# A 3x3 convolution by Winograd rows: four products in five lower halves, and the differences on VectorE

## The chip, the core and the metric

The kernel runs on one core of a Trainium2 chip. Its time is the device time of one execution in microseconds (us). Of the engines, TensorE (PE) multiplies matrices from SBUF into PSUM; VectorE (DVE), ScalarE (ACT) and GpSimd (POOL) work elementwise; SyncE (SP) issues all transfers between HBM and SBUF, which 16 DMA engines carry. A "half" below is 32 of the 64 output rows of a pair of images.

## The reference

The output is the 3x3 convolution of 16 images of 64 channels and 64x64 pixels with 128 filters, padded with one row and column of zeros, all in float32:

```python
x_pad = np.pad(x, ((0, 0), (0, 0), (1, 1), (1, 1)), mode='constant')
...
output[b, co] += weight[co, ci, kh, kw] * x_pad[b, ci, kh:kh+h, kw:kw+w]
```

## The kernel before

Two images make a pair: their 2 x 64 channels fill the 128 partitions, so eight pairs (`p` = 0 to 7) are worked on, each in two halves (`h` = 0 the upper, 1 the lower), sixteen halves in a row (the loop at the end of the function). Each half gives two blocks of 8 row pairs: the block F (rows 16 to 31 in the upper half, 32 to 47 in the lower) and the block G (rows 0 to 15, or 48 to 63).

Rows are combined as in Winograd's scheme for two output rows of a three-tap filter. With two neighbouring input rows b (even) and c (odd), the kernel makes in float16 the sums b+c ("ss", `sums`, L108), the differences c-b ("dd", `diffs`, L115) and the differences of the rows on both sides ("ee", `outers`, L125). The weights are combined once, at the start, into seven sets (`Wt`, L88 on): G0, G1, G2 are the three filter rows, HP and HM half of (G0 + G2) plus and minus half of G1, G01 is G0-G1, G21 is G2-G1. A product is six matrix multiplications: three column taps for each of the two images (`mms`, L162); each is of 64 input channels, and the two images' run side by side.

Block F of each half takes four products (HP on ss, HM on dd, G0 on ee, G2 on ee). Block G takes five: G1 on ss, and four on "xh", a plain float16 copy of 17 rows that ScalarE makes (`cast`, L138): G01 and G2 into one PSUM tile, G21 and G0 into another. So a half has nine products, 54 multiplications.

The four PSUM tiles of a half are pf1, pg1, pf2 and pg2, and these are all there are: the next half uses the same four again in the same order. ScalarE copies the first products out to the output rows (L247, L249, L251); when the later products have been added in PSUM, VectorE adds or subtracts the tile to those rows (L258 frees pg2, L259 frees pf1, L260 frees pf2), and ScalarE copies pg1 (L261).

The order on each engine is that of the program's text (`keep` holds every instruction in its place). GpSimd makes sums, differences and outers of the half after next (`transforms`, called with n + 2); only the very first half's are VectorE's. ScalarE makes the cast of the next half after its three copies. The buffers of "ss" and "dd" are four, those of "xh" three, and those of "ee" two, one for each pair.

SBUF holds eleven "homes" of one 64x64 row image a partition (L51 on). All inputs are loaded at the start, by SyncE, in the order of the pairs. The outputs of a pair take two homes, some of them the pair's own input home, some that of an earlier output, which must have been stored (`O_HOME`). Home 6, the second of pair 2 and of pair 3, is such a one.

`stores` (L213) issues the stores, all on SyncE's queue. Nothing is stored before half (2, 0) is done; then four parts and pairs 0, 1 and 2 follow, and from pair 3 on each pair after its lower half, both images in one transfer (`store_both`). Pair 5 is an exception: its first image goes in one transfer, rows 0 to 56 of the second in another, and its last seven rows in two, of 124 channels and of 4.

Of the kernel before, what the change touches and what calls it, by code (L numbers as in the profile page):

```python
# [9 lines left out]
F16 = mybir.dt.float16  # L10
# [5 lines left out]
def kernel(  # L16
# [12 lines left out]
    nc = tc.nc  # L29
    B, CI, H, W = x.shape  # L30
    CO = weight.shape[0]
    assert H == 64 and W == 64 and CI == 64 and CO == 128 and B == 16
    NP = B // 2
    RB = 8

    keep = tc.keep_in_program_order
# [8 lines left out]
    cpool = ctx.enter_context(tc.tile_pool(name="cpool", bufs=3))  # L45
# [7 lines left out]
    xs = [homes[:, k, :, :] for k in X_HOME]  # L53

    def out_homes(p):
        lo, hi = O_HOME[p]
        return homes[:, lo : hi + 1 : hi - lo, :, :]
# [29 lines left out]
    G0, G1, G2, G21, G01, HP, HM = range(7)  # L87
# [4 lines left out]
    def wrow(i):  # L92
        return Wt[:, i, :, :].rearrange("p t c -> p (t c)")
# [8 lines left out]


    F_BLK, G_BLK = (1, 2), (0, 3)
    C_ROW = (0, 47)
    tr = {}

    def sums(eng, p, h):  # L108
        v = xs[p].rearrange("p (j i) c -> p j i c", i=2)
        t = tpool.tile([128, 16, W], F16, tag="ss", name="ss")  # L110
        j = 16 * h
        keep(eng.tensor_add(t, v[:, j : j + 16, 0, :], v[:, j : j + 16, 1, :]))  # L112
        return t

    def diffs(eng, p, h):  # L115
        v = xs[p].rearrange("p (j i) c -> p j i c", i=2)
        t = tpool.tile([128, RB, W], F16, tag="dd", name="dd")
        j = RB * F_BLK[h]
        keep(eng.tensor_sub(t, v[:, j : j + RB, 1, :], v[:, j : j + RB, 0, :]))  # L119
        return t  # L120

# [3 lines left out]
    def outers(eng, p, h):  # L125
        if h == 0:
            ees[p] = epool.tile([128, 32, W], F16, tag="ee", name="ee")
        lo, hi = (16, 33) if h == 0 else (33, 48)
        keep(
            eng.tensor_sub(  # L130
                ees[p][:, lo - 16 : hi - 16, :],
                xs[p][:, lo - 1 : hi - 1, :],
                xs[p][:, lo + 1 : hi + 1, :],
            )
        )
        return ees[p]

    def cast(p, h):  # L138
        t = cpool.tile([128, 17, W], F16, tag="xh", name="xh")
        keep(nc.scalar.copy(t, xs[p][:, C_ROW[h] : C_ROW[h] + 17, :]))  # L140
        return t

    def transforms(eng, p, h):
        return sums(eng, p, h), diffs(eng, p, h), outers(eng, p, h)

    xh = {}
    keep(nc.scalar.mul(g0h, wps[0], 0.5))  # L147
    keep(nc.scalar.copy(wrow(G0), wps[0]))
# [2 lines left out]
    keep(nc.scalar.copy(wrow(G1), wps[1]))  # L151
    s0 = sums(nc.vector, 0, 0)
    keep(nc.vector.scalar_tensor_tensor(wrow(HM), wps[1], -0.5, th, MULT, ADD))
    d0 = diffs(nc.vector, 0, 0)
    xh[0, 0] = cast(0, 0)
    keep(nc.vector.tensor_sub(wrow(G01), wps[0], wrow(G1)))
    keep(nc.scalar.copy(wrow(G2), wps[2]))
    keep(nc.vector.tensor_sub(wrow(G21), wps[2], wrow(G1)))
    tr[0, 0] = s0, d0, outers(nc.vector, 0, 0)
    tr[0, 1] = transforms(nc.gpsimd, 0, 1)  # L160

    def mms(tiles, terms, start, stop):  # L162
        n = 3 * len(terms)
        i = 0
        for wi, src, row in terms:
            for kw in (1, 0, 2):
                c_lo, c_hi = max(0, 1 - kw), min(W, W + 1 - kw)
                lo, hi = 0, RB
                at, step, rows = row
                while at + step * lo < 0:  # L170
                    lo += 1
                while at + step * (hi - 1) > rows - 1:
                    hi -= 1
                first, last = at + step * lo, at + step * (hi - 1)
                for b2 in range(2):
                    p0 = 64 * b2
                    keep(
                        nc.tensor.matmul(  # L178
                            tiles[:, b2, lo:hi, c_lo:c_hi],
                            Wt[p0 : p0 + 64, wi, kw, :],  # L180
                            src[
                                p0 : p0 + 64,
                                first : last + 1 : step,
                                c_lo + kw - 1 : c_hi + kw - 1,
                            ],
                            start=start and i == 0,
                            stop=stop and i == n - 1,
                            skip_group_check=not start,
                        )
                    )  # L190
                i += 1

    def acc():
        return psum.tile([128, 2, RB, W], F32, tag="acc", name="acc")

    halves = [(p, h) for p in range(NP) for h in range(2)]

    def store(p, b2, lo=0, hi=H, c=0, n=CO):
        keep(
            nc.sync.dma_start(  # L200
                out[2 * p + b2, c : c + n, lo:hi, :], out_homes(p)[c : c + n, b2, lo:hi, :]
            )
        )

    def store_both(p):
        pair = out[2 * p : 2 * p + 2, :, :, :].rearrange("b c h w -> c b h w")
        keep(nc.sync.dma_start(pair, out_homes(p)))

    FEW = 57

    def stores(p, h):  # L213
        if (p, h) == (2, 0):
            store(2, 1, 0, 32)
            store(0, 0)
        elif (p, h) == (2, 1):
            store(2, 1, 32, H)
            store(0, 1)
            store_both(1)  # L220
            store(2, 0)
        elif (p, h) == (5, 1):
            store(5, 0)
            store(5, 1, 0, FEW)
            store(5, 1, FEW, H, 0, 124)
            store(5, 1, FEW, H, 124, 4)
        elif p > 2 and h == 1:
            store_both(p)

    for n, (p, h) in enumerate(halves):  # L230
        if n + 2 < len(halves):
            tr[halves[n + 2]] = transforms(nc.gpsimd, *halves[n + 2])
        if h == 0:
            both = out_homes(p)
            ov = both.rearrange("p b (j i) c -> p b j i c", i=2)
        ss, dd, ee = tr.pop((p, h))
        xc = xh.pop((p, h))
        jf, jg = RB * F_BLK[h], RB * G_BLK[h]
        sf, sg = jf - 16 * h, jg - 16 * h
        g_at = 2 * jg - C_ROW[h]  # L240


        f0, f1 = (ov[:, :, jf : jf + RB, i, :] for i in range(2))
        g0, g1 = (ov[:, :, jg : jg + RB, i, :] for i in range(2))
        pf1, pg1, pf2, pg2 = acc(), acc(), acc(), acc()
        mms(pf1, [(HP, ss, (sf, 1, 16))], True, True)
        keep(nc.scalar.copy(f1, pf1))  # L247
        mms(pg1, [(G1, ss, (sg, 1, 16))], True, True)
        keep(nc.scalar.copy(g1, pg1))  # L249
        mms(pf2, [(HM, dd, (0, 1, RB))], True, True)  # L250
        keep(nc.scalar.copy(f0, pf2))  # L251
        if n + 1 < len(halves):
            xh[halves[n + 1]] = cast(*halves[n + 1])
        mms(pg2, [(G01, xc, (g_at, 2, 17)), (G2, xc, (g_at + 2, 2, 17))], True, True)
        mms(pf1, [(G0, ee, (16 * h, 2, 32))], False, True)
        mms(pg1, [(G21, xc, (g_at + 1, 2, 17)), (G0, xc, (g_at - 1, 2, 17))], False, True)
        mms(pf2, [(G2, ee, (16 * h + 1, 2, 32))], False, True)
        keep(nc.vector.tensor_add(g1, pg2, g1))  # L258
        keep(nc.vector.tensor_add(f0, pf1, f0))  # L259
        keep(nc.vector.tensor_sub(f1, f1, pf2))  # L260
        keep(nc.scalar.copy(g0, pg1))  # L261
        stores(p, h)


# [28 lines left out]
```

## Time and profile before

| what | value |
|---|---|
| median of 3 runs | 126.45 us (126.12 to 126.69) |
| the profiled execution | 126.43 us |
| its span, first to last instruction | 124.56 us |
| PE busy | 96.4 us, 77% of the span |
| DVE busy | 64.0 us, 51% |
| ACT busy | 81.3 us, 65% |
| POOL busy | 90.4 us, 73% |
| queue of SyncE's transfers | 50.63 MB, 96.6% of 16 engines' span |
| HBM | 17.07 MB read, 33.55 MB written |

The span is what the profile shows of the execution; the time around it belongs to the execution, not to an instruction. "Busy" is the time in which an engine had an instruction at work. In the profile's lines "out<-in" names the program's tiles, L178 is line 178 of the kernel, and a line like "9.44 2.34 POOL L112" in a timeline gives start, duration, engine and line. Instructions of VectorE, ScalarE and GpSimd overlap a little with the next one of their engine, so the spacing of their starts is somewhat below the duration shown. Where the prediction speaks of the packet list, it means the single DMA packets in the trace, with start, duration and size; packets of 4 bytes signal the end of a transfer's share on one DMA engine.

### The profile page before, as it was taken

To read this page: it belongs to the slowest core of one execution; us is meant where nothing else is said; L and a number is where in the kernel's file an instruction comes from. 1 tells how busy PE (TensorE), PEld (TensorE's weight loads), DVE (VectorE), ACT (ScalarE), POOL (GpSimd) and SP (SyncE) were. 2 spreads that over 40 slices of the span, in tenths; PEclk is the share of its full clock that TensorE was granted. 3 is DMA by queue.
4 is the path that set the end of the run, shared out by engine and by line. 5 is a ranking of instruction groups with operands and counts; after the bars stand their busy time and mean duration, and the time that the engine had idled before them with its cause. 6 is when DMAs were issued, how large, how long until landed. Compare 5 with 4: busy or idle time off the path is not lost.

```text
span 124.6 us, 2115 instructions
## 1 busy us (share of the span) xinstructions
PE 96.4 (77%) x873; PEld 50.0 (40%) x873; DVE 64.0 (51%) x56; ACT 81.3 (65%) x86; POOL 90.4 (73%) x52
## 2 busy tenths in 40 slices
PE   0339999999999999969999999999999996000000
PEld 0213555555545544534555555555555552000000
DVE  0199666473939381907384938566573939000000
ACT  4456688888797947749979796988888793000000
POOL 2209999999999999999999999999999600000000
PEclk9999999999999999999999999999999999855555
DMA  4999999999999999999999999999999999999981
GB/s 123 359 455 426 426 447 421 416 442 426 426 431 421 408 445 424 431 429 426 431 434 413 437 421 434 416 431 426 437 421 427 419 390 422 421 421 442 437 374 68
DMA packets 3954, 50.77 MB, mean 408 GB/s; under 512 B 360, under 2 KB 488, under 8 KB 744
## 3 DMA queue, kind: packets, MB, share of 16 engines
q1 hardware_dynamic: 3944, 50.63, 96.6%
q8 instruction: 7, 0.11, 0.3%
q14 instruction: 3, 0.02, 0.0%
HBM read 17.07 MB, written 33.55 MB: 406 GB/s over the span
## 4 chain that ended last, share of the span: by engine, by line
PE 68%; DMA 11%; DVE 3%; ACT 2%; SPq 0%; issue 0%; ACTq 0%
PE acc L178 68%; DMA out_dram<-homes 6%; DMA homes<-in_x_dram 5%; DVE homes L260 2%; DVE ss L112 1%; ACT homes L247 1%; ACT homes L249 1%; SPq L66 0%; ACTq L247 0%; SPq L200 0%
## 5 line engine op out<-in xcount | busy, mean ns | idle before, releaser
L178 PEld LDWEIGHTS <-Wt 64*128 64x128 f16 x864 | 49.0, 96 | 49.9 <-issue 6.8
L178 PE MATMUL acc<-xh,Wt 64*128 64x504 f16 (+3 forms) x384 | 46.3, 372 | 0.2
L112 POOL TENSOR_TENSOR ss<-homes 128x1024 f16<-128x1024 f32 x15 | 35.4, 2360 | 5.1 <-DMA homes<-in_x_dram 5.1
L258 DVE TENSOR_TENSOR homes<-acc,homes 128x1024 f32<-128x1024 f32 x16 | 19.6, 1224 | 35.3 <-PE acc L178 23.9
L130 POOL TENSOR_TENSOR ee<-homes 128x960 f16<-128x960 f32 (+1 forms) x15 | 35.2, 2349 | 0.0
L178 PE MATMUL acc<-ee,Wt 64*128 64x504 f16 (+1 forms) x192 | 26.5, 377 | 1.2 <-ACT homes L247 1.1
L178 PE MATMUL acc<-ss,Wt 64*128 64x504 f16 (+1 forms) x192 | 24.9, 392 | 2.6 <-DVE ss L112 2.6
L261 ACT COPY homes<-acc 128x1024 f32<-128x1024 f32 x16 | 16.3, 1016 | 9.7 <-PE acc L178 9.7
L247 ACT COPY homes<-acc 128x1024 f32<-128x1024 f32 x16 | 16.2, 1012 | 9.7 <-PE acc L178 5.2
L119 POOL TENSOR_TENSOR dd<-homes 128x512 f16<-128x512 f32 x15 | 20.0, 1337 | 0.0
L260 DVE TENSOR_TENSOR homes<-homes,acc 128x1024 f32<-128x1024 f32 x16 | 19.5, 1219 | 1.0 <-PE acc L178 0.2
L259 DVE TENSOR_TENSOR homes<-acc,homes 128x1024 f32<-128x1024 f32 x16 | 19.4, 1214 | 0.0
L140 ACT CAST xh<-homes 128x1088 f16<-128x1088 f32 x16 | 17.9, 1119 | 0.0
L251 ACT COPY homes<-acc 128x1024 f32<-128x1024 f32 x16 | 16.5, 1030 | 0.3 <-PE acc L178 0.3
L249 ACT COPY homes<-acc 128x1024 f32<-128x1024 f32 x16 | 16.3, 1017 | 0.3 <-PE acc L178 0.3
L178 PE MATMUL acc<-dd,Wt 64*128 64x504 f16 (+1 forms) x96 | 13.9, 392 | 0.0
L101 PE MATMUL wp<-homes 128*128 128x128 f16 x9 | 1.2, 310 | 4.5 <-POOL homes L84 4.5
L149 DVE SCALAR_TENSOR_TENSOR homes<-wp,homes 128x384 f32<-128x384 f32 x1 | 0.6, 557 | 5.6 <-ACT homes L147 5.6
L130 DVE TENSOR_TENSOR ee<-homes 128x1088 f16<-128x1088 f32 x1 | 2.8, 2812 | 0.0
L101 PEld LDWEIGHTS <-homes 128*128 128x128 f16 x9 | 0.9, 159 | 4.5 <-POOL homes L84 4.5
L84 POOL CAST homes<-homes 128x576 f16<-128x576 f32 x1 | 0.7, 662 | 2.4 <-DMA homes<-in_weight_dram 2.4
L85 ACT CAST homes<-homes 128x576 f16<-128x576 f32 x1 | 0.7, 671 | 1.7 <-DMA homes<-in_weight_dram 1.7
(17 smaller groups left out, 8.2 us busy)
## 6 DMA issues: line engine op xcount, KB each, us to landing
out_dram<-homes SPq DMA_DIRECT2D x5, 4096.0 KB, 20.9
homes<-in_x_dram SPq DMA_DIRECT2D x7, 2048.0 KB, 30.3
out_dram<-homes SPq DMA_DIRECT2D x4, 2048.0 KB, 16.4
out_dram<-homes SPq DMA_DIRECT2D x2, 1024.0 KB, 6.5
out_dram<-homes SPq DMA_DIRECT2D x1, 1824.0 KB, 20.5
homes<-in_x_dram SPq DMA_DIRECT2D x1, 1088.0 KB, 5.8
homes<-in_x_dram SPq DMA_DIRECT2D x1, 960.0 KB, 7.6
homes<-in_weight_dram SPq DMA_DIRECT2D x1, 288.0 KB, 2.9
```

The costliest lines, as they stand in the source:

```text
L112: keep(eng.tensor_add(t, v[:, j : j + 16, 0, :], v[:, j : j + 16, 1, :]))
L119: keep(eng.tensor_sub(t, v[:, j : j + RB, 1, :], v[:, j : j + RB, 0, :]))
L130: eng.tensor_sub(ees[p][:, lo - 16 : hi - 16, :], xs[p][:, lo - 1 : hi - 1, :], xs[p][:, lo + 1 : hi + 1, :],)
L140: keep(nc.scalar.copy(t, xs[p][:, C_ROW[h] : C_ROW[h] + 17, :]))
L178: nc.tensor.matmul(tiles[:, b2, lo:hi, c_lo:c_hi], Wt[p0 : p0 + 64, wi, kw, :], src[p0 : p0 + 64, first : last + 1 : step, c_lo + kw - 1 : ...
L247: keep(nc.scalar.copy(f1, pf1))
L249: keep(nc.scalar.copy(g1, pg1))
L251: keep(nc.scalar.copy(f0, pf2))
L258: keep(nc.vector.tensor_add(g1, pg2, g1))
L259: keep(nc.vector.tensor_add(f0, pf1, f0))
L260: keep(nc.vector.tensor_sub(f1, f1, pf2))
L261: keep(nc.scalar.copy(g0, pg1))
```

## The change

In the lower halves of pairs 2 to 6 (`FOUR`) block G takes four products as block F does: HP on ss, HM on its own differences, and G0 and G2 on outer differences of rows 47 to 64. These outer differences lie in the "xh" tile, and VectorE makes them (`last_outers`), with the last row as a plain copy. ScalarE makes no cast for such a half, copies all four first products out, and VectorE adds or subtracts all four tiles.

The differences c-b of all halves are VectorE's now, and no longer GpSimd's. They are queued for the next half (`others`) ahead of the work of the present one, so ahead of its additions and subtractions.

The stores of pair 5 are two, one an image, and so are those of pairs 6 and 7; pairs 3 and 4 keep one transfer for both images.

```diff
+    FOUR = ((2, 1), (3, 1), (4, 1), (5, 1), (6, 1))
...
+    def last_outers(eng, p):
+
+        t = cpool.tile([128, 17, W], F16, tag="xh", name="xh")
+        keep(eng.tensor_sub(t[:, 0:15, :], xs[p][:, 47:62, :], xs[p][:, 49:64, :]))
+        keep(eng.tensor_copy(t[:, 15, :], xs[p][:, 62, :]))
+        return t
+
     def transforms(eng, p, h):
-        return sums(eng, p, h), diffs(eng, p, h), outers(eng, p, h)
-
+        return sums(eng, p, h), outers(eng, p, h)
+
+    def others(p, h):
+
+        dd[p, h] = [diffs(nc.vector, p, F_BLK[h])]
+        if (p, h) in FOUR:
+            dd[p, h].append(diffs(nc.vector, p, G_BLK[h]))
+            xh[p, h] = last_outers(nc.vector, p)
...
-        elif (p, h) == (5, 1):
-            store(5, 0)
-            store(5, 1, 0, FEW)
-            store(5, 1, FEW, H, 0, 124)
-            store(5, 1, FEW, H, 124, 4)
+        elif p in (5, 6, 7) and h == 1:
+            store(p, 0)
+            store(p, 1)
         elif p > 2 and h == 1:
             store_both(p)
...
+        four = (p, h) in FOUR
+        if n + 1 < len(halves):
+            others(*halves[n + 1])
...
-        mms(pg1, [(G1, ss, (sg, 1, 16))], True, True)
+        mms(pg1, [(HP if four else G1, ss, (sg, 1, 16))], True, True)
...
-        if n + 1 < len(halves):
+        if four:
+            mms(pg2, [(HM, ds[1], (0, 1, RB))], True, True)
+            keep(nc.scalar.copy(g0, pg2))
+        if n + 1 < len(halves) and halves[n + 1] not in FOUR:
             xh[halves[n + 1]] = cast(*halves[n + 1])
-        mms(pg2, [(G01, xc, (g_at, 2, 17)), (G2, xc, (g_at + 2, 2, 17))], True, True)
+        if not four:
+            mms(pg2, [(G01, xc, (g_at, 2, 17)), (G2, xc, (g_at + 2, 2, 17))], True, True)
         mms(pf1, [(G0, ee, (16 * h, 2, 32))], False, True)
-        mms(pg1, [(G21, xc, (g_at + 1, 2, 17)), (G0, xc, (g_at - 1, 2, 17))], False, True)
+        if four:
+            mms(pg1, [(G0, xc, (0, 2, 16))], False, True)
+        else:
+            mms(pg1, [(G21, xc, (g_at + 1, 2, 17)), (G0, xc, (g_at - 1, 2, 17))], False, True)
         mms(pf2, [(G2, ee, (16 * h + 1, 2, 32))], False, True)
-        keep(nc.vector.tensor_add(g1, pg2, g1))
-        keep(nc.vector.tensor_add(f0, pf1, f0))
-        keep(nc.vector.tensor_sub(f1, f1, pf2))
-        keep(nc.scalar.copy(g0, pg1))
+        if four:
+            mms(pg2, [(G2, xc, (1, 2, 16))], False, True)
+            keep(nc.vector.tensor_add(f0, pf1, f0))
+            keep(nc.vector.tensor_add(g0, pg1, g0))
+            keep(nc.vector.tensor_sub(f1, f1, pf2))
+            keep(nc.vector.tensor_sub(g1, g1, pg2))
+        else:
+            keep(nc.vector.tensor_add(g1, pg2, g1))
+            keep(nc.vector.tensor_add(f0, pf1, f0))
+            keep(nc.vector.tensor_sub(f1, f1, pf2))
+            keep(nc.scalar.copy(g0, pg1))
         stores(p, h)
```

More of the change, by code (lines that the diff above doesn't have):

```diff
@@ L113, in sums, with diffs @@
         return t
-    def diffs(eng, p, h):
+    def diffs(eng, p, blk):
         v = xs[p].rearrange("p (j i) c -> p j i c", i=2)
         t = tpool.tile([128, RB, W], F16, tag="dd", name="dd")
-        j = RB * F_BLK[h]
+        j = RB * blk
         keep(eng.tensor_sub(t, v[:, j : j + RB, 1, :], v[:, j : j + RB, 0, :]))
@@ L141, in cast @@
         return t
-    def transforms(eng, p, h):
-        return sums(eng, p, h), diffs(eng, p, h), outers(eng, p, h)
+    def last_outers(eng, p):
[3 more added lines that the diff above has]
+        return t
+    def transforms(eng, p, h):
+        return sums(eng, p, h), outers(eng, p, h)
[4 more added lines that the diff above has]
+            xh[p, h] = last_outers(nc.vector, p)
+    dd = {}
     xh = {}
@@ L153 @@
     keep(nc.vector.scalar_tensor_tensor(wrow(HM), wps[1], -0.5, th, MULT, ADD))
-    d0 = diffs(nc.vector, 0, 0)
+    dd[0, 0] = [diffs(nc.vector, 0, F_BLK[0])]
     xh[0, 0] = cast(0, 0)
@@ L158 @@
     keep(nc.vector.tensor_sub(wrow(G21), wps[2], wrow(G1)))
-    tr[0, 0] = s0, d0, outers(nc.vector, 0, 0)
+    tr[0, 0] = s0, outers(nc.vector, 0, 0)
     tr[0, 1] = transforms(nc.gpsimd, 0, 1)
@@ L196, with store @@
     halves = [(p, h) for p in range(NP) for h in range(2)]
[L198 to L203, printed above, removed]
+    def store(p, b2, lo=0, hi=H):
+        keep(nc.sync.dma_start(out[2 * p + b2, :, lo:hi, :], out_homes(p)[:, b2, lo:hi, :]))
     def store_both(p):
@@ L207, in store_both @@
         keep(nc.sync.dma_start(pair, out_homes(p)))
-    FEW = 57
     def stores(p, h):
@@ L235 @@
             ov = both.rearrange("p b (j i) c -> p b j i c", i=2)
-        ss, dd, ee = tr.pop((p, h))
-        xc = xh.pop((p, h))
+        ss, ee = tr.pop((p, h))
+        xc, ds = xh.pop((p, h)), dd.pop((p, h))
         jf, jg = RB * F_BLK[h], RB * G_BLK[h]
@@ L247 @@
         keep(nc.scalar.copy(f1, pf1))
-        mms(pg1, [(G1, ss, (sg, 1, 16))], True, True)
+        mms(pg1, [(HP if four else G1, ss, (sg, 1, 16))], True, True)
         keep(nc.scalar.copy(g1, pg1))
-        mms(pf2, [(HM, dd, (0, 1, RB))], True, True)
+        mms(pf2, [(HM, ds[0], (0, 1, RB))], True, True)
         keep(nc.scalar.copy(f0, pf2))
-        if n + 1 < len(halves):
+        if four:
+            mms(pg2, [(HM, ds[1], (0, 1, RB))], True, True)
+            keep(nc.scalar.copy(g0, pg2))
+        if n + 1 < len(halves) and halves[n + 1] not in FOUR:
             xh[halves[n + 1]] = cast(*halves[n + 1])
-        mms(pg2, [(G01, xc, (g_at, 2, 17)), (G2, xc, (g_at + 2, 2, 17))], True, True)
+        if not four:
+            mms(pg2, [(G01, xc, (g_at, 2, 17)), (G2, xc, (g_at + 2, 2, 17))], True, True)
         mms(pf1, [(G0, ee, (16 * h, 2, 32))], False, True)
-        mms(pg1, [(G21, xc, (g_at + 1, 2, 17)), (G0, xc, (g_at - 1, 2, 17))], False, True)
+        if four:
+            mms(pg1, [(G0, xc, (0, 2, 16))], False, True)
+        else:
+            mms(pg1, [(G21, xc, (g_at + 1, 2, 17)), (G0, xc, (g_at - 1, 2, 17))], False, True)
         mms(pf2, [(G2, ee, (16 * h + 1, 2, 32))], False, True)
-        keep(nc.vector.tensor_add(g1, pg2, g1))
-        keep(nc.vector.tensor_add(f0, pf1, f0))
-        keep(nc.vector.tensor_sub(f1, f1, pf2))
-        keep(nc.scalar.copy(g0, pg1))
+        if four:
[9 more added lines that the diff above has]
+            keep(nc.scalar.copy(g0, pg1))
         stores(p, h)
```

## The prediction

> **What bounds the kernel now.** I read the page's slices first, then the busy time by stretches, then the waits of SyncE, which issues every transfer, and last the timelines of VectorE and GpSimd.
>
> ```profile
> DMA  4999999999999999999999999999999999999981
> GB/s 123 359 455 426 426 447 421 416 442 426 426 431 421 408 445 424 431 429 426 431 434 413 437 421 434 416 431 426 437 421 427 419 390 422 421 421 442 437 374 68
> ```
>
> The 16 DMA engines are full from the second slice to the last but one, at 420 to 430 GB/s: 50.6 MB cannot end much earlier. TensorE ends long before, at 105. What follows it, by stretches (columns: stretch, length, busy time of PE, PEld, DVE, ACT, POOL, then granted clock, DMA share, GB/s):
>
> ```profile
> 80.00:100.00 20.00, 20.00 (x190) 10.68 (x188) 13.33 (x12) 16.32 (x18) 18.49 (x10) 1.00 1.01 427
> ...
> 107.00:121.00 14.00, 0.00 (x0) 0.00 (x0) 0.00 (x0) 0.00 (x0) 0.00 (x0) 0.55 0.99 421
> ```
>
> In the last 14 us the transfers alone work. SyncE's last issue, and the line's time to landing in the window that holds this issue alone:
>
> ```profile
> 106.18 0.40 SPq L207 DMA_DIRECT2D out_dram<-homes  x1
> ...
> DMA to landing us min/median/max: 17.5/17.5/17.5
> ```
>
> The last pair's store is issued at 106.18 and lands at 123.7. With an empty queue it would need 1.0 us to its first packet (the weight load: issue 0.74, first packet 1.75), 9.9 us for 4.19 MB at 425 GB/s and 0.3 to land: 11.3. So it stands 6.2 us in the queue: compute has a reserve of **6.2 us**, and beyond it each us of delay is a us of time. Landing to span's end is 0.8 us; the profiled execution took 126.43, its span 124.56, so 1.87 lies around it. Time = last issue + 11.3 + 0.8 + 1.9 = last issue + **14.0**, but not under 126.4. The median of the runs is 126.45, so nothing has to be rescaled.
>
> Compute runs at 11.5 us a pair of images (issues at 60.26, 71.65, 83.16, 94.67, 106.18), and TensorE sets it: 5.76 us a half (first products at 75.90 and 81.66), nine products of 0.64.
>
> **What the port costs.** The change gives VectorE subtractions with both inputs in SBUF, while GpSimd goes on adding SBUF rows. The trace has this just once, at the start:
>
> ```profile
> 9.44 2.34 POOL L112 TENSOR_TENSOR ss<-homes 128x1024 f16<-128x1024 f32 x1 [5.07 <-DMA homes<-in_x_dram]
> 10.12 2.81 DVE L130 TENSOR_TENSOR ee<-homes 128x1088 f16<-128x1088 f32 x1
> 11.75 2.32 POOL L119 TENSOR_TENSOR dd<-homes 128x512 f16<-128x512 f32 x1
> ...
> 18.52 1.28 POOL L119 TENSOR_TENSOR dd<-homes 128x512 f16<-128x512 f32 x1
> ```
>
> VectorE's 1088 elements, at the pace of its 1024 at 6.98 (1.22 us) worth 1.3, took 2.81: GpSimd's ss ended at 11.78, and VectorE ended 1.15 later. GpSimd's dd of 512, elsewhere 1.28, took 2.32 and ended 1.14 after VectorE. So each stood still for the other's whole instruction. The evictions (one input in PSUM) are 1.22 beside a GpSimd that never rests, so they are free of it.
>
> **The change part by part.**
>
> *GpSimd* loses its 15 differences, 1.23 each from start to start, and keeps sums (2.33) and outers (2.45 upper, 2.19 lower half). It takes 9.3 us a pair instead of 11.8, runs ahead of TensorE and is then held by the two "ee" buffers: the tile of pair p+2 is free when TensorE has read pair p's, near the end of that pair's lower half. From about there it works a burst of four operations, some 2.3 us each.
>
> *TensorE* saves one product in nine in five halves: 5 x 0.64 = 3.2 us, lower halves of 5.1. Worth nothing alone, as it only adds to the reserve.
>
> *ScalarE* drops five casts (1.0 each) and moves a copy forward; its 81 busy us fall, and nothing waits for it longer.
>
> *VectorE* per pair: 7 evictions instead of 6, at 1.14 from start to start (79.38, 80.52) = 8.0; three differences of 512 at 0.60 (8.59 to 9.19) = 1.8; the outer difference of 960, between 0.60 (512) and 1.14 (1024), nearest 1024: 1.07; the copy of 64 elements, which no row shows, between 0 and 0.54 (the 384-element operation at 9.66 took 0.55): I take 0.15. Sum 11.0, against TensorE's 5.76 + 5.12 = 10.9. VectorE turns from half idle to as loaded as TensorE, before any port wait.
>
> *The order.* The block for the next half (two differences, outer, copy: 0.60 + 0.60 + 1.07 + 0.15 = 2.4) is queued ahead of this half's evictions. These give back the PSUM tiles: the lower half's first product needs the tile that the upper half's second eviction frees. So a port wait in the block goes straight to TensorE.
>
> *One pair worked out*, from TensorE's start of the upper half at 0. The lower half's four evictions before it begin once five of its eight products and ScalarE's third copy are in, 1.6 before 0: 4 x 1.14 ends at 3.0. Now the block wants the port. GpSimd's burst began near 0, its operations end near 2.4 and 4.7, so the block waits 1.7. How often does it wait? In the one handover above VectorE won against a GpSimd instruction already up (11.75), so I take it to hold the port through its own back-to-back instructions, which start 0.08 before the one ahead ends (9.19 against 9.27): **one wait per block**. Bounds: no wait, and one before each of three subtractions. Block from 4.7 to 7.1; TensorE's nine products, with 1 us of waits for late tiles, are ready at 7.0; two evictions to 9.5 with handovers; lower half 5.1: **14.6 us a pair instead of 11.5**.
>
> *Sum.* Five blocks x 3.1 = 15.5. The first pair's lower half pays 0.4 (its single difference behind GpSimd). Given back: ScalarE now waits 1.85 and 2.51 us at pair 3 for stores to free its home; compute that comes later finds them landed: -4.4. Last issue: 106.2 + 15.5 + 0.4 - 4.4 = 117.7. Time 117.7 + 14.0 = **131.7**.
>
> The Trainium skill, "SBUF — State Buffer", section "Who interferes with whom", says a VectorE instruction with two SBUF inputs and a GpSimd one that reads SBUF exclude each other, whoever issues first holding the port for the whole instruction. The rows at 9.44 to 11.75 agree. Read strictly, first come first served, it speaks for the alternating rival below, 155.7 instead of 131.7.
>
> *Stores.* Pairs 6 and 7 split in two cost 0.40 us more of SyncE's issuing, behind which nothing waits; same bytes in the same 16 KB packets. Pair 5 loses its 128 packets of 1792 bytes, 74 ns each in the packet list, on four engines; 100 to 104 ran at 392 GB/s, not 425: (1 - 392/425) x 4 = 0.3 us of the queue. That counts only if the queue still sets the end. The first stores (40.83) come about 1 to 2 us later; the queue has loads until 42.1, so it idles at most that long, in a run that is late anyway.
>
> **The rivals.**
> 1. *Alternating.* GpSimd gets the port between VectorE's subtractions. Block: 4.7 to 5.3, GpSimd to 7.5, 8.1, GpSimd to 10.4, outer and copy to 11.7; two evictions 14.0, lower half 19.1: +7.6 a pair. 106.2 + 38 + 1.9 (the same in the first pair) - 4.4 = 141.7, time 155.7. TensorE then idles 7 us a pair. The clock fell 3.5 us after its last product (104.9, 108.4), and until 12.8 products started every 0.43 instead of 0.21 us for 4.5 us: +2.2 x 5, 166.7 at worst. For it: VectorE had waited longest in that one handover. Against: it needs a gap between VectorE's instructions.
> 2. *More than one wait in some blocks*: between 135 and 146.
> 3. *No wait that matters, not slower.* If the block finds the port free it ends at 5.4, and TensorE's own 7.0, two evictions to 7.9 and 5.1 make 13.0 a pair: 106.2 + 7.5 - 4.4 = 109.3, up to 111.7 if the 4.4 is not given back whole. It decides at 112.4 (106.2 + 6.2): below that, the queue hides all: 126.4. For it: GpSimd has 20% less to do, and the wait of 1.7 hangs on its burst beginning when I say.
> 4. *Faster.* As 3, and the engines end evener. In the packet list ten DMA engines end at 120.7 to 121.7 and six at 122.7 to 123.4; the four with the small packets, 32 x 74 ns = 2.4 us each, are among the late. Without, they end up to 2 us earlier and the others 8 x (611 - 545 ns) = 0.5 later: at best 125.5. Against: two late engines carry none of these packets.
>
> **How the numbers follow.** One wait per block: 0.45, own range 127.5 (1.7 x 5 = 8.5 less, but not under the queue) to 135 (copy and outer at their upper bounds, 0.5 x 5, and a late tile more). Rival 2: 0.12. Alternating: 0.15. Hidden: 0.18. Faster: 0.10. Measurement can tell about 0.5%, 0.6 us. Faster 0.10, same 0.18, slower 0.72. The range runs from rival 4 to rival 2's end, 125.5 to 146; the alternating rival is left out.
>
> **What would show it.** Right: VectorE's differences of 512 show 0.7 to 3 us, the first in each block longest; GpSimd's operations grow beside them; TensorE idles 2 to 3 us ahead of each lower half of pairs 2 to 6; issues of pair stores 14 to 15 us apart, DMA below 9 in the slices between. Wrong: stores still 11.5 to 13 apart and DMA full (rival 3); three long subtractions a block and the clock down between halves (rival 1). The price of a wait is wrong if GpSimd isn't bursting at the end of a lower half.

## The result and the profile after

The changed kernel takes 159.58 us (median of 6 runs, 159.09 to 160.59); the kernel before, run beside it, 126.38. The ratio is **1.263** (95% interval 1.259 to 1.266): 33 us slower, where 131.7 was predicted with a range of 125.5 to 146. The profiled execution took 160.59 us, its span 158.6. The time lies between the two values of the alternating rival: 155.7, and 166.7 with the clock at its worst.

The page of the changed kernel, engines and slices of 4 us:

```profile
PE 109.0 (69%) x843; PEld 47.5 (30%) x843; DVE 118.7 (75%) x91; ACT 77.9 (49%) x81; POOL 78.7 (50%) x37
...
POOL 2069999999993299302993019930098000000000
PEclk9999999999965999759998589985799969999955
DMA  5999999999701989999999801993009940697996
```

The DMA row, full from end to end before, now has four holes. The granted clock (PEclk) falls in each of the five four-product halves, also in the second of them, where the transfers still fill the queue (both slices of 63 to 71 us show DMA 9 and PEclk 7 and 5). VectorE's busy time went from 64.0 to 118.7 us. Its work in instructions did not grow like that, as two groups of the same page show (busy us, then mean ns of one):

```profile
L120 DVE TENSOR_TENSOR dd<-homes 128x512 f16<-128x512 f32 x21 | 35.8, 1723 | 0.0
...
L147 DVE TENSOR_TENSOR xh<-homes 128x960 f16<-128x960 f32 x5 | 14.3, 2861 | 0.0
```

A difference of 512 that takes 0.68 us unhindered takes 1.72 in the mean, an outer difference of 960 takes 2.86 instead of 1.15. The profile books a wait for the port as busy time of the waiting instruction; there is no idle time to see.

One block in the changed kernel's timeline (start, duration, engine, line), with TensorE's upper half begun at 94.80:

```profile
94.47 2.50 POOL L131 TENSOR_TENSOR ee<-homes 128x1088 f16<-128x1088 f32 x1 [9.97 <-PE acc L194]
96.93 2.35 POOL L113 TENSOR_TENSOR ss<-homes 128x1024 f16<-128x1024 f32 x1
97.76 4.69 DVE L120 TENSOR_TENSOR dd<-homes 128x512 f16<-128x512 f32 x2
99.24 2.66 POOL L131 TENSOR_TENSOR ee<-homes 128x960 f16<-128x960 f32 x1
101.86 2.78 POOL L113 TENSOR_TENSOR ss<-homes 128x1024 f16<-128x1024 f32 x1
102.37 3.29 DVE L147 TENSOR_TENSOR xh<-homes 128x960 f16<-128x960 f32 x1
105.58 0.18 DVE L148 CAST xh<-homes 128x64 f16<-128x64 f32 x1
105.69 1.21 DVE L284 TENSOR_TENSOR homes<-acc,homes 128x1024 f32<-128x1024 f32 x1
106.95 2.74 PE L194 MATMUL acc<-ss,Wt 64*128 64x512 f16 x12 [5.07 <-DVE homes L284]
109.49 2.77 PE L194 MATMUL acc<-dd,Wt 64*128 64x512 f16 x12
```

GpSimd's burst begins at 94.47, when TensorE releases the "ee" tile. VectorE asks for its first difference at 97.76 and gets the port when GpSimd's ss ends (99.28); then GpSimd's outer runs, then the second difference, then GpSimd's next sum, then VectorE's outer. The engines take turns. From the moment when a VectorE instruction is due to the end of the GpSimd instruction ahead of it, the three waits are 1.5, 2.1 and 2.2 us. The block takes 8.0 us (97.76 to 105.76) instead of 2.4. Then one eviction (L284) frees the tile that TensorE has waited 5.07 us for.

The end of the chain of waits in order of time, in the same stretch (start, us, what), shows these to be the path:

```profile
97.90 2.14 PE acc L194 x18
100.04 0.04 DVEq L285
100.07 2.38 DVE dd L120
102.45 3.21 DVE xh L147
105.66 0.10 DVE xh L148
105.76 1.15 DVE homes L284
106.91 0.05 issue
106.95 7.69 PE acc L194 x30
```

The last of the five blocks is an experiment that the changed kernel makes by itself. GpSimd has only one instruction left then, and the outer difference and the copy do not wait:

```profile
118.07 4.70 DVE L120 TENSOR_TENSOR dd<-homes 128x512 f16<-128x512 f32 x2
119.54 2.67 POOL L131 TENSOR_TENSOR ee<-homes 128x960 f16<-128x960 f32 x1
122.69 1.15 DVE L147 TENSOR_TENSOR xh<-homes 128x960 f16<-128x960 f32 x1
123.76 0.18 DVE L148 CAST xh<-homes 128x64 f16<-128x64 f32 x1
```

### The profile page after: what moved, and what is told of

Same layout as the page of the kernel before. It is cut to its first block, busy times and chain, and to the rows that moved or that the text cites. A ratio compares the mean times of both kernels' runs of the same rounds, so it can differ in the third digit from the quotient of the medians.

```text
span 158.6 us, 2069 instructions
## 1 busy us (share of the span) xinstructions
PE 109.0 (69%) x843; PEld 47.5 (30%) x843; DVE 118.7 (75%) x91; ACT 77.9 (49%) x81; POOL 78.7 (50%) x37
## 4 chain that ended last, share of the span: by engine, by line
PE 28%; DVE 23%; issue 0%; DVEq 0%
PE acc L194 28%; DVE xh L147 5%; DVE dd L120 5%; DVE homes L280 3%; DVE homes L282 3%; DVE homes L284 3%; DVE homes L281 3%; DVE homes L286 1%; DVE homes L285 1%; DVE xh L148 0%; DVEq L285 0%
## 5 line engine op out<-in xcount | busy, mean ns | idle before, releaser
L194 PEld LDWEIGHTS <-Wt 64*128 64x128 f16 x834 | 46.6, 103 | 92.9 <-DVE homes L284 28.2
L131 POOL TENSOR_TENSOR ee<-homes 128x960 f16<-128x960 f32 (+1 forms) x15 | 39.5, 2632 | 35.4 <-PE acc L194 35.4
L194 PE MATMUL acc<-ss,Wt 64*128 64x504 f16 (+1 forms) x192 | 31.4, 458 | 28.8 <-DVE homes L284 25.4
L194 PE MATMUL acc<-xh,Wt 64*128 64x512 f16 (+1 forms) x324 | 40.6, 378 | 1.5 <-DVE homes L282 1.5
L113 POOL TENSOR_TENSOR ss<-homes 128x1024 f16<-128x1024 f32 x15 | 38.9, 2595 | 5.2 <-DMA homes<-in_x_dram 5.2
L120 DVE TENSOR_TENSOR dd<-homes 128x512 f16<-128x512 f32 x21 | 35.8, 1723 | 0.0
L194 PE MATMUL acc<-dd,Wt 64*128 64x504 f16 (+1 forms) x126 | 22.9, 495 | 1.5 <-DVE homes L281 1.5
L287 ACT COPY homes<-acc 128x1024 f32<-128x1024 f32 x11 | 11.1, 1013 | 19.0 <-PE acc L194 19.0
L284 DVE TENSOR_TENSOR homes<-acc,homes 128x1024 f32<-128x1024 f32 x11 | 13.4, 1216 | 5.2 <-PE acc L194 5.2
L147 DVE TENSOR_TENSOR xh<-homes 128x960 f16<-128x960 f32 x5 | 14.3, 2861 | 0.0
L286 DVE TENSOR_TENSOR homes<-homes,acc 128x1024 f32<-128x1024 f32 x11 | 13.3, 1212 | 0.4
L285 DVE TENSOR_TENSOR homes<-acc,homes 128x1024 f32<-128x1024 f32 x11 | 13.3, 1210 | 0.0
L141 ACT CAST xh<-homes 128x1088 f16<-128x1088 f32 x11 | 12.2, 1107 | 0.0
L282 DVE TENSOR_TENSOR homes<-homes,acc 128x1024 f32<-128x1024 f32 x5 | 6.1, 1213 | 0.0
L281 DVE TENSOR_TENSOR homes<-homes,acc 128x1024 f32<-128x1024 f32 x5 | 6.0, 1210 | 0.0
## 6 DMA issues: line engine op xcount, KB each, us to landing
out_dram<-homes SPq DMA_DIRECT2D x3, 4096.0 KB, 15.3
```

The costliest lines, as they stand in the source:

```text
L131: eng.tensor_sub(ees[p][:, lo - 16 : hi - 16, :], xs[p][:, lo - 1 : hi - 1, :], xs[p][:, lo + 1 : hi + 1, :],)
L147: keep(eng.tensor_sub(t[:, 0:15, :], xs[p][:, 47:62, :], xs[p][:, 49:64, :]))
L194: nc.tensor.matmul(tiles[:, b2, lo:hi, c_lo:c_hi], Wt[p0 : p0 + 64, wi, kw, :], src[p0 : p0 + 64, first : last + 1 : step, c_lo + kw - 1 : ...
```

## The experiments

The theory: each VectorE instruction of the block that needs the port waits for one GpSimd instruction. Rivals: the wait is not what costs, but VectorE's load, the stores, or TensorE's clock.

**Parts of the change.** All differences on VectorE, no lower half with four products (the rest as changed):

```diff
-    FOUR = ((2, 1), (3, 1), (4, 1), (5, 1), (6, 1))
+    FOUR = ()
```

> The change without its four-product halves: all differences of 512 on VectorE, one a half, and the new stores; every lower half works as before. Theory (port): VectorE and GpSimd take turns at a shared SBUF read port, and a VectorE subtraction waits for the whole GpSimd operation ahead of it. One difference a half then shows 0.7 to 3 us, but VectorE has 2 us idle a half, so pair stores stay 11.5 to 11.8 us apart, the last is issued between 107 and 110, inside the reserve of 6.2 us, and the time is 126 to 127. Rival (any such subtraction costs its wait in full): 14 differences at 1 to 2 us each late, 135 or more.

127.06 us, ratio 1.006 (1.003 to 1.009), at the upper edge of what was expected. Its differences take 0.68 to 2.71 us, so they do wait, and yet the pair stores stay 11.4 to 11.5 apart: VectorE has room. The stores of the change in the kernel before:

```diff
+        elif p in (5, 6, 7) and h == 1:
+            store(p, 0)
+            store(p, 1)
```

> The kernel before with the change's stores alone: pairs 5, 6 and 7 as one transfer an image, no separate rows. Theory: the bytes are the same and the queue is full, 125.8 to 126.8; the six late DMA engines at the end become two or three. Rival (the separate rows evened out the ends): 127 to 128.

126.72 us, 1.003 (1.000 to 1.005), as expected in time. But in the packet list the last transfer still ends late on six DMA engines (123.2 to 124.3, the other ten by 122.5), not on two or three, so rival 4 of the prediction, where the separate rows cause the late ends, is not borne out. Neither part holds the 33 us; that leaves the blocks. With three of them:

```diff
+    FOUR = ((4, 1), (5, 1), (6, 1))
```

> The change with three four-product halves, those of pairs 4, 5 and 6, instead of five. Theory (each block pays its own three port waits and a cold TensorE): in the changed kernel pair stores came, against the differences alone, 8.2 us later after the first block's upper half and then 8.8, 8.8 and 5.9 later a block; three blocks give about 25 us on a last issue of 106.6, time 143 to 147. Rival (most of the loss is a consequence of the early blocks, which empty the store queue): 130 to 138.

143.41 us, 1.139 (1.134 to 1.145), as expected. Against the kernel without blocks, the changed one issues its pair stores 17.0 us later after two blocks, and 8.8, 8.8 and 5.9 more with the next three; the last is the cheap one.

**The waits counted.** One subtraction of 1024 in place of two of 512, which should leave two waits of three (cut; the single differences have two buffers here instead of four, and the merged ones have one):

```diff
-            dd[p, h].append(diffs(nc.vector, p, G_BLK[h]))
+            t = mpool.tile([128, 16, W], F16, tag="dm", name="dm")
+            keep(nc.vector.tensor_sub(t, v[:, 16:32, 1, :], v[:, 16:32, 0, :]))
+            dd[p, h] = [t[:, 0:RB, :], t[:, RB:16, :]]
```

> The change with the two differences of 512 of a four-product half made by one VectorE subtraction of 1024; same output. Theory (port, one wait for each subtraction): a block has two waits instead of three, so each of five blocks is about 2.6 us shorter: pair stores 17 to 18 us apart instead of 20.3, time 145 to 148. Rival (VectorE keeps the port through a block, and its length comes from something else) or rival (the fourth eviction and the tile order make the pair long): 159, as nothing but 0.1 us an instruction is saved.

157.12 us, 1.241 (1.236 to 1.246): a miss by 9 us. The timeline of this kernel tells why:

```profile
95.21 2.61 DVE L161 TENSOR_TENSOR dm<-homes 128x1024 f16<-128x1024 f32 x1
...
97.74 3.17 DVE L149 TENSOR_TENSOR xh<-homes 128x960 f16<-128x960 f32 x1
99.86 3.25 POOL L115 TENSOR_TENSOR ss<-homes 128x1024 f16<-128x1024 f32 x1
100.84 2.33 DVE L150 CAST xh<-homes 128x64 f16<-128x64 f32 x1
```

There are still three waits: the copy of 64 elements, which has one input, now comes when GpSimd has an instruction up, and takes 2.33 us, the length of GpSimd's turn. In this kernel's last block, with GpSimd done, it takes 0.18. The Trainium skill, "SBUF — State Buffer", section "Who interferes with whom", says that a copy can enter a mode that takes both ports, and then contends with GpSimd as a subtraction of two inputs does. The 2.33 against 0.18 agree with that. So the same kernel with that copy on ScalarE:

```diff
-        keep(eng.tensor_copy(t[:, 15, :], xs[p][:, 62, :]))
+        keep(nc.scalar.copy(t[:, 15, :], xs[p][:, 62, :]))
```

> One subtraction of 1024 a block, as in the run before it, and the copy of 64 elements on ScalarE instead of VectorE. In that run the copy took 2.33 us in a block, 0.18 where GpSimd was done: it had taken over the third wait. Theory (one wait for each VectorE instruction that needs the port, as long as GpSimd has one queued): two waits a block are left, four of the five blocks are 2.2 us shorter, pair stores 16 to 17.5 apart, time 146 to 149. Rival (what a block waits is fixed by GpSimd's burst of four and moves on to the next instruction, whichever it is): 156 to 158.

146.11 us, 1.154 (1.149 to 1.159), as expected: taking 0.18 us of work a block off VectorE gains 11 us. Its block has two long instructions, then goes straight to the evictions:

```profile
86.86 2.61 DVE L161 TENSOR_TENSOR dm<-homes 128x1024 f16<-128x1024 f32 x1
...
89.39 3.17 DVE L149 TENSOR_TENSOR xh<-homes 128x960 f16<-128x960 f32 x1
...
92.48 1.21 DVE L290 TENSOR_TENSOR homes<-acc,homes 128x1024 f32<-128x1024 f32 x1
```

**No wait at all.** VectorE keeps every instruction of the changed block, but GpSimd cannot begin its burst earlier: VectorE, as the block's last act, writes 64 elements into the "ee" tile that GpSimd is to fill next (GpSimd then overwrites them), and GpSimd's sum goes ahead of the block.

```diff
+        if gated:
+            s = sums(nc.gpsimd, *nx)
         if n + 1 < len(halves):
             others(*halves[n + 1])
+        if gated:
+            ees[nx[0]] = epool.tile([128, 32, W], F16, tag="ee", name="ee")
+            keep(nc.vector.tensor_copy(ees[nx[0]][:, 0, :], xs[p][:, 62, :]))
+            tr[nx] = s, outers(nc.gpsimd, *nx, made=True)
```

> The change with GpSimd held still while VectorE makes a block: VectorE ends each block with a copy of 64 elements into the ee tile that GpSimd writes next, so that GpSimd's burst starts after the block; same output, one more small copy a block. Theory (port): from the second block on the subtractions show 0.7 and 1.15 us, a pair takes 13 to 13.6 us, the last issue comes at 110 to 114, and the time is 126 to 128. Rival (the extra VectorE work and the tile order make the pair long, not the port): above 150.

128.41 us, 1.015 (1.012 to 1.019): 31 of the 33 us are gone, with the same work on VectorE and one copy more.

```profile
76.82 1.28 DVE L120 TENSOR_TENSOR dd<-homes 128x512 f16<-128x512 f32 x2
...
78.02 1.15 DVE L147 TENSOR_TENSOR xh<-homes 128x960 f16<-128x960 f32 x1
79.09 0.18 DVE L148 CAST xh<-homes 128x64 f16<-128x64 f32 x1
79.19 0.18 DVE L259 CAST ee<-homes 128x64 f16<-128x64 f32 x1
79.30 1.21 DVE L292 TENSOR_TENSOR homes<-acc,homes 128x1024 f32<-128x1024 f32 x1
79.55 2.51 POOL L131 TENSOR_TENSOR ee<-homes 128x1088 f16<-128x1088 f32 x1 [2.76 <-DVE ee L259]
...
82.69 2.23 DVE L120 TENSOR_TENSOR dd<-homes 128x512 f16<-128x512 f32 x1
```

The block is 2.5 us, and GpSimd waits 2.76 for it. With the waits, TensorE's long idle times went, and with them its slow halves (PEclk stays at 9 until compute ends), so the 31 us hold both. What now sets the pair is VectorE's load: the 11.0 us a pair of the prediction, and 1.5 by which the single difference at 82.69 still waits, make 12.5; the stores are 12.55 apart, and VectorE is busy 20.00 of 20.00 us from 66 to 86. The last store is issued at 113.12, just past the 112.4 at which compute takes over from the queue.

That does not yet make 128.41, which is 0.4 above the expected range: 113.12 + 14.0 is 127.1. The rest lies in the queue of transfers. This is the DMA row of this kernel, in slices of 3.2 us:

```profile
DMA  4999999999999399999999999999999999989991
```

The first store is issued at 43.44 instead of 40.83, and from 42 to 44 the DMA share is 0.12, where the kernel before has 0.96. That is 1.7 us of transfers lost, so the queue ends at about 126.4 + 1.7 = 128.1 (an estimate), after compute.

The table puts these kernels beside one another (waits in a block in the middle of the run; pair: spacing of the pair stores there):

| kernel | waits in a block | pair, us | time, us |
|---|---|---|---|
| changed | 3 | 20.3 | 159.58 |
| one subtraction of 1024 | 3 | 19.1 | 157.12 |
| the same, copy on ScalarE | 2 | 17.0 | 146.11 |
| GpSimd held back | 0 | 12.55 | 128.41 |

**The load on another engine.** All these operations on GpSimd, VectorE with evictions alone:

```diff
-            dd[p, h].append(diffs(nc.vector, p, G_BLK[h]))
-            xh[p, h] = last_outers(nc.vector, p)
+            dd[p, h].append(diffs(nc.gpsimd, p, G_BLK[h]))
+            xh[p, h] = last_outers(nc.gpsimd, p)
```

(and the same for the single differences)

> The change with all differences, those of the five four-product halves too, on GpSimd instead of VectorE; same products, same evictions, same output. No VectorE subtraction with two SBUF inputs is left after the start. Theory (port): GpSimd works 15.4 us a pair (9.3, three differences of 1.23, an outer of 2.2, a small copy) and sets the pace, the last issue at 119 to 123, time 133 to 137, some 24 us below the change although the slower engine does the work. Rival (four products, the fourth eviction and the order of tiles cost the time): 150 or more.

141.62 us, 1.123 (1.119 to 1.126): 18 us faster than the change although the slower engine does the work, and after the start no VectorE instruction waits for the port. The pace is as forecast: GpSimd is busy 20.00 of 20.00 us from 60 to 80 and from 80 to 100, and the pair stores are 15.3 us apart. TensorE gets it through ScalarE, whose first copy overwrites the pair's input rows and so waits for GpSimd's block:

```profile
93.57 0.26 POOL L148 CAST xh<-homes 128x64 f16<-128x64 f32 x1
93.68 1.01 ACT L259 COPY homes<-acc 128x1024 f32<-128x1024 f32 x1 [3.31 <-POOL xh L147]
```

It missed its 133 to 137 in the last issue, which came at 127.67 and not at 119 to 123. Added as the prediction adds, 106.2 + 5 x 3.9 - 4.4 is 121.3, the middle of the forecast; without the 4.4 us "given back", on which more below, it is 125.7. Where the other 2 us come from is open.

**The clock.** After about 5 us without a product, the lower half's products start every 0.43 us (12 in the 2.74 us at 106.95, two side by side) and not every 0.21; the half takes 8.16 us (106.95 to 115.11) instead of 5.1. The granted clock is 1.00 until 106, 0.58 from 106 to 107 and 0.50 from 107 to 113; the last product before had ended at 101.88. The Trainium skill, "TensorE: Matmul & The Clock Gate", section "Part 1: The HAM clock gate", gives an idle window of some 3.4 us after which products run at half rate; the trace agrees, with a fall 4.1 to 5.1 us after the last product. To take this away, 42 products whose result is overwritten were put ahead of each of the five halves, into the tile pg1:

```diff
+        if four:
+            for _ in range(7):
+                mms(pg1, [(HP, ss, (sg, 1, 16))], True, True)
```

> The change with 42 more multiplications ahead of each four-product half, into the PSUM tile of its second product, which ScalarE has already emptied; they are overwritten, the output is the same. They fill TensorE's idle time of 5 us there and nothing else: VectorE, GpSimd and the port are as in the change. Theory (part of the loss is the clock, which falls to half in that idle time): a four-product half took 7.3 to 8.2 us in the change and takes 5.3 to 5.6 now, some 2.7 us less in four halves and 1.9 in the last, time 145 to 150. Rival (the port waits are all of the loss, the slow products are hidden behind VectorE): 158 to 162.

181.28 us, 1.432 (1.427 to 1.437): a miss, since the added products waited for VectorE as well. The second try put them into pg2, on the thought that this tile comes free earlier:

```diff
+                mms(pg2, [(HP, ss, (sg, 1, 16))], True, True)
```

> The 42 added multiplications ahead of each four-product half again, this time into the tile of its fourth product, which is the one that ScalarE empties 1 us after the half before; they are overwritten, the output is the same. The run before it put them into a tile that VectorE empties, so they came after the wait (181.3 us) and showed only that a half at full clock takes 5.3 us. Theory (the clock is a part of the loss): the added products start about 1 us after the upper half's last and end with the port's block, the half after them takes 5.3 to 5.6 instead of 8.2 (7.3 the last), time 145 to 150. Rival (the port waits are all of the loss): 158 to 162.

179.95 us, 1.428 (1.422 to 1.434), a miss for the same reason. Its timeline of TensorE:

```profile
94.71 8.07 PE L194 MATMUL acc<-ss,Wt 64*128 64x512 f16 x54 [4.88 <-DVE homes L287]
102.62 1.46 PE L194 MATMUL acc<-dd,Wt 64*128 64x512 f16 x12
```

The expectation was wrong about the tile: in both tries the products that came first, into pg1 or into pg2, waited for VectorE's first eviction (L287 in these kernels), so neither try could fill the gap. The half behind the added products takes 5.4 us, against 8.2 in the changed kernel: about 2.8 us of the 8.8 of a block belong to the clock. That is a comparison of halves in two traces; no run separates it by its time.

**Is there a gain left?** GpSimd held back, and one block fewer, to stay within the reserve:

```diff
+    FOUR = ((3, 1), (4, 1), (5, 1), (6, 1))
```

> GpSimd held still during VectorE's blocks, and four four-product halves, pairs 3 to 6. With five, the first stores came at 43.4 instead of 40.8, and the transfers had a hole of 2 us. Theory (what was left of the loss is that hole): first stores at 41 to 42, no slice of the middle below 9, pair stores 12.5 apart, last issue 110 to 112.5, time 126.4 to 127.2. Rival (the longer pairs of 12.5 us are what costs): 128 or more.

126.81 us, 1.005 (1.003 to 1.007), as expected: the last store is issued at 111.26, and the hole is all but gone (DMA share 0.87 from 42 to 44). The same with the stores of the kernel before:

> GpSimd held still during VectorE's blocks, four-product halves in pairs 3 to 6, and the stores of the kernel before, with pair 5's separate rows. Theory (with no waits at the port the queue of transfers sets the end, and the change's stores were the rest of the difference of 0.5%): 126.1 to 126.6, no difference from the kernel before. Rival (the longer pairs or the first stores, 0.8 us later, cost it): 126.8 or more.

127.36 us, 1.008 (1.005 to 1.010), where 126.1 to 126.6 was expected. So the 0.5% is not from the stores; the first stores are issued 0.8 us later (41.6 against 40.83), which was not tried by itself, and the cause stays open. None of these kernels is faster than the kernel before.

## Why the prediction was wrong

**What held.** *The reserve and the formula.* Time = last issue + 14.0 gives 160.65 for the changed kernel (last issue 146.65), against 160.59 of the profiled execution; 143.6, 141.7 and 146.1 for three blocks, GpSimd alone and the copy on ScalarE, against medians of 143.41, 141.62 and 146.11. It falls short by 1.3 for the held-back kernel, where the hole in the queue sets the end. *The path.* The block ahead of the evictions goes straight to TensorE. *When the port is wanted.* The block was to ask 3.0 us after the upper half's start, and asks 2.96 after it (94.80 to 97.76); GpSimd's operations were to end near 2.4 and 4.7, and end 2.2 and 4.5 after it; the first wait was put at 1.7 and is 1.5. *VectorE's load* of 11.0 a pair is what the held-back kernel leaves when its one wait of 1.5 is taken off. *Costs taken at nothing*, or nearly: the stores (0.3%) and the differences of the other halves (0.6% with the stores), while VectorE has room.

**The step that failed: "one wait per block".** From the single handover at 11.75, where VectorE went ahead of a GpSimd instruction that was up, the prediction concluded that VectorE holds the port through its back-to-back instructions. But VectorE had waited since 10.12 there, and so that row fits turns just as well, which the prediction itself noted as the rival's support. The runs show turns: after each VectorE instruction that needs the port, a waiting GpSimd instruction runs to its end. That VectorE's instructions follow one another with no gap does not help, so the argument against the rival was void. With waits of 1.5, 2.1 and 2.2 us the block ends 10.96 after the upper half's start instead of 7.1.

**Three sizes in the same sum.** *Two evictions.* The lower half's first product was said to need the tile that the second eviction frees; it starts right after the first (106.95, after L284 ended at 106.90, while L285 was still at work). L284 empties pg2, so the four tiles are not used again "in the same order", as the description of the kernel before has it; the next product waits for L285, which empties pf1 (seen at 126.25). That takes 1.2 us off: 12.15 instead of the 13.4 that 10.96 would give by the prediction's own 2.4. *The lower half of 5.1* was taken at full clock; after the longer idle it is 8.16, 3.1 more. Together 12.15 + 8.16 = 20.3 us a pair, which is the spacing of the trace, where 14.6 was forecast.

*The 4.4 us given back* are ScalarE's two waits for stores in the kernel before, 1.85 and 2.51, taken in full off the sum. In the changed kernel ScalarE indeed waits for no store. But in the kernel before TensorE waited for ScalarE only once, 1.1 us at 55.75, and was busy 18.61 of 20.00 us from 40 to 60; and in the kernel without blocks, where ScalarE waits for no store either, the last store comes at 106.64, not ahead of 106.18. So about 1 us was there to be given back, and no run shows 4.4.

Two small sums of the working are off, with no bearing on the result: 1.0 + 9.9 + 0.3 is 11.2, not 11.3, and 8.5 us less than 131.7 is 123.2, so the lower end of that case was the queue's 126.4, not 127.5.

**The small copy** was put between 0 and 0.54 by its size. Its price has two values: 0.18, or up to 2.33 when GpSimd has an instruction up. In the changed kernel's first block it is 2.19 (at 44.37).

**The range.** The rival was named, with its mechanism, its 7.6 us a pair and the clock's 2.2, but was given 0.15 and left out. One handover that fits both cases does not carry odds of three to one, and the larger case belonged in the range.

## What to carry to other kernels

Count the instructions on VectorE that share the port with a busy GpSimd, not their microseconds: here each waits for a whole GpSimd instruction, some 2.2 us even for a copy worth 0.18. If they must stand ahead of an eviction that TensorE waits for, merge them, give the small ones to ScalarE, or hold GpSimd back until they are done, which here took 31 of 33 us away. And after an idle of some 5 us TensorE's next half took 8.2 us instead of 5.4. Holding GpSimd back also moved the first stores here, by 2.6 us, and the hole in the queue of transfers, not the last issue, then set the end.

## What the runs showed of the hardware

- A copy with one input, 64 elements a partition, float32 to float16, waits for GpSimd as a subtraction of two inputs does: 2.33 us against 0.18.
- VectorE and GpSimd take turns instruction by instruction, also where VectorE's instructions are queued with no gap. GpSimd's blocked ones grow only by VectorE's turn: the outer from 2.2 to 2.66, the sum from 2.35 to 2.78 beside differences of 512, 3.25 beside an operation of 960.
- Neither wait shows as idle time in the profile; it is seen only as a longer duration against the same form elsewhere.
